# Row sums and root steps kept in PSUM, GpSimd's order written out in one stage, and the opening's order of work changed, in a three-layer float32 block on one core

## The chip, the cores and the metric

The kernel runs on one core of a Trainium2 chip. The metric is the device time of one execution in microseconds. Three executions of the kernel before took 1303.06, 1309.24 and 1313.09 us; their median is 1309.24 us. A further execution was recorded by the hardware profiler.

The core has five engines that run side by side: PE (TensorE, matrix products, which write to the accumulator memory PSUM), DVE (VectorE), ACT (ScalarE), POOL (GpSimd, which works in the main on-chip memory SBUF alone) and SP (SyncE, which here only issues the loads and stores). Each takes its own instructions strictly one after the other, so an instruction that waits holds up all that is queued behind it on its engine.

## The reference, cut to what matters

512 tokens of width 1024 pass through one block of a first model and two layers of a second, all in float32:

```
h = rms_norm(x);  proj = h @ w_in                       # 3 kinds of keys and values, queries, gates
y_attn = (compressed + selected + window attention) @ w_attn_br
y_conv = silu(layer_norm(conv31(a * sigmoid(gate)))) @ w_conv_br
x = x + (g_a * y_attn + g_b * y_conv) @ w_out           # g_a, g_b: sigmoid gates, 2 x 1024 wide
x = x + (silu(conv3(u_a)) * conv3(u_v)) @ w_down        # u = rms_norm(x) @ w_up, 2 x 2816 wide
x = rms_norm(x)
layer 0: x = x + gate * even_mixer(rms_norm(x) * (1 + scale) + shift)   # dense + latent attention
layer 1: x = x + gate * odd_mixer(rms_norm(x) * (1 + scale) + shift)    # window of 128, sinks
out = rms_norm(x)
```

Every rms_norm and layer_norm needs, for each token, the sum of 1024 (or 512) squares and 1/sqrt of it.

## The kernel before, in words

**Layout.** The tokens lie along the free dimension: x is held as eight tiles X[0..7] of 128 features by 512 tokens. A tile of 512 float32 in each of the 128 partitions fills one PSUM bank; there are eight banks, in the pools pg (2), ps (2), pt (3) and po (1).

**Products.** PE multiplies numbers that are split in two: a rounded high part (ACT copies it) and a low part, the difference (POOL or DVE subtracts). `wload` (line 100) loads a weight tile over SP's queue into a raw buffer (pools t and wr), makes its high part at line 110 on ACT and its low part at line 111 on POOL or DVE; the list `wpools` says which raw pool and which engine come next in turn. `mm3` (line 121) then issues three products for each of the eight steps along the contracted dimension: low weight times high x (line 124), high times low (125), high times high (126), all added up in one bank.

**Squares and roots.** `Squares` (line 198) takes eight tiles. ACT squares each one into an SBUF tile (line 222), DVE adds them up in an SBUF buffer z one behind (lines 212 and 215), and `sums` lets PE add the 128 features of each token by products with a column of ones (line 232): one product for 128 tokens of the sum, and one for the last square. DVE reads these few columns at line 183 and `newton` (line 160) makes 1/sqrt in eight more small instructions (lines 164 to 173), each of which needs the one before. All of its operands lie in SBUF. `row_bcast` (line 186) spreads the result over the partitions with PE (line 189). There are twelve such roots: one for the first norm (line 346), one for the layer_norm (698), one for the second norm (722), two by halves of the tokens in the first model's last product (853), two for queries and keys (923), one for the latents (942), two in layer 0's last product (1127), two in layer 1's (1232).

**What sets the order.** The program is traced in the order of the text, and a scheduler decides each engine's order by simulated times and free buffers. `in_order(...)` (line 281) pins the named engines to the order of the text; `after_root()` and `after()` put a block's instructions behind a given one on its engine. Loads are issued by SP in the scheduler's order and wait in that queue for a free buffer.

**The opening** (lines 321 to 355): for each k ACT makes the high part of X[k], DVE the low part; four tiles of the first weights w0 are loaded in between; ACT's order is pinned. Then ACT squares the eight tiles. PE, pinned as well, does the two products pkv[0] and pkv[1], then half of pkb[0] (four steps), the sums of squares, the rest of pkb[0], the broadcast of the root, and pkb[1]. Line 437 takes pkb out of its banks, in the text behind `windows(tkv[0])`, which is a row of copies on ACT, DVE and POOL. The next products (line 453, `natural`) need a free ps bank, which pkb holds, and the weights wv, eight tiles whose low parts are made by POOL, DVE, POOL in turn (line 425).

**The gates** (lines 643 to 684): behind the first model's attention, PE multiplies by the sixteen gate weights, each two tiles of `wload` with the low part on POOL. In the same stage the convolution's 31 taps go on: three channel tiles on DVE, and tile 0 on POOL, one addition at line 488 for each tap, of a copy that ACT makes at line 487. Sixteen taps of tile 0 are left for this stage, spread over fourteen gates in the text. PE and DVE are pinned here, POOL is not.

**By halves** (`by_halves`, line 796): in the last product of each model's layers, tokens 0 to 255 are finished first and their root is made while PE works on tokens 256 to 511. Evacuations of the second half stand behind the first half's root on DVE.

Of the kernel before, what the change touches and what calls it, by code (L numbers as in the profile page):

```python
# [18 lines left out]
D = 1024  # L19
# [24 lines left out]
def build(ctx, tc, I, out):  # L44
# [49 lines left out]
    V.memset(ones, 1.0)  # L94


    wpools = [[("t", "wh", "wl", G), ("t", "wh", "wl", V), ("wr", "wh", "wl", G)]]
# [22 lines left out]

    def mm3(ps, ls, rs, start=True, stop=True):
        n = len(ls)
        for i, ((lh, ll), (rh, rl)) in enumerate(zip(ls, rs)):
            PE.matmul(ps, ll, rh, start=start and i == 0, stop=False)  # L124
            PE.matmul(ps, lh, rl, start=False, stop=False)  # L125
            PE.matmul(ps, lh, rh, start=False, stop=stop and i == n - 1)  # L126
# [32 lines left out]

    def newton(x):  # L160
        n = x.shape[1]
        y = new("s", (128, 20))[:, :n]
        t = new("s", (128, 20))[:, :n]
        V.tensor_scalar(y.bitcast(I32), x.bitcast(I32), -0.5, float(0x5F3759DF), op0=OP.mult, op1=OP.add)


        V.tensor_mul(t, y, y)
        V.scalar_tensor_tensor(t, t, -0.5 * 0.375, x, op0=OP.mult, op1=OP.mult)
        V.scalar_tensor_tensor(y, t, 1.5 * 0.375, y, op0=OP.add, op1=OP.mult)
        V.tensor_mul(t, y, y)  # L170
        V.scalar_tensor_tensor(t, t, 64.0 / 9, x, op0=OP.mult, op1=OP.mult)
        V.scalar_tensor_tensor(t, t, -10.0 / 3, t, op0=OP.add, op1=OP.mult)
        root[:] = [V.scalar_tensor_tensor(y, t, 5.0, y, op0=OP.add, op1=OP.mult)]
        return y

# [4 lines left out]

    def rsqrt(src, scale, eps):
        x = new("s", (128, 20))[:, :src.shape[1]]
        V.tensor_scalar(x, src, scale, eps, op0=OP.mult, op1=OP.add)
        return newton(x)

# [7 lines left out]
    def to_sbuf(ps, tag="R"):  # L193
        t = new("r", tag=tag)
        V.tensor_copy(t, ps)
        return t

    class Squares:


        def __init__(self, a=0, b=512):
            self.c = slice(a, b)
            self.acc = self.last = None
# [15 lines left out]

        def add(self, src, scale=1.0):  # L220
            t = new("p")
            A.activation(t[:, self.c], src[:, self.c], AF.Square, scale=scale)  # L222
            self.put(t)

        def sums(self, bank="ps"):
            st = new(bank)
            n = (self.c.stop - self.c.start) // 128
            for x in (self.acc, self.last):
                for i in range(n):

                    a = self.c.start + 128 * i
                    PE.matmul(st[:, i:i + 1], x[:, a:a + 128], ones[:, 0:1], start=x is self.acc and i == 0,  # L232
                              stop=x is self.last, skip_group_check=True)
            return st[:, 0:n]

# [106 lines left out]
    with in_order("PE"):  # L342
        for b in range(2):
            mm3(pkv[b], w0[8 * b:8 * b + 8], xg)
        mm3(pkb[0], wk[0][:4], xg[:4], True, False)
        r1 = rsqrt(total.sums("pt"), 1.0 / D, EPS)
        mm3(pkb[0], wk[0][4:], xg[4:], False, True)
        R1 = to_sbuf(row_bcast(r1, "pt"))
# [3 lines left out]
    for b in range(2):  # L352
        t = new("p")
        V.tensor_mul(t, pkv[b], R1)
        tkv.append(t)
# [67 lines left out]
    KB = []  # L423
    with after_root():
        wv = wsplit(I["w_v"], KT, 280, ("m", "h"))
    nc.sync.dma_start(vec[:, 8:NVEC], I["vec"][:, 8:NVEC])
# [3 lines left out]
    w2h, w2l = split(w2r, shape=(128, 128), p="z")  # L430
    w2k, w2v = [(w2h[:, i:i + 64], w2l[:, i:i + 64]) for i in (0, 64)]
    with after_root():
        ZK = windows(tkv[0], cv("pek", 0, 16))
    tkb = []
    for b in range(2):
        tkb.append(new("p"))
        V.tensor_mul(tkb[b], pkb[b], R1)
    with after_root():
# [244 lines left out]
    with in_order("PE", "DVE"):  # L683
        gates(0, 7, 0, 90)
        total = Squares()
# [5 lines left out]
        PE.matmul(mp, ones, total.last, start=False, stop=True)  # L691
        total = Squares()
        for c in range(4):
# [23 lines left out]
    for m in range(KT):  # L717
# [3 lines left out]
        total.add(X[m])  # L721
    R2 = to_sbuf(row_bcast(rsqrt(total.sums(), 1.0 / D, EPS), "po"), "R'")

# [122 lines left out]
    for th, c in by_halves(I["w_dn"], 18, 22, ACTV[18:], down, "t", ws):  # L846
# [5 lines left out]
        V.scalar_tensor_tensor(v[:, 2:4], st[:, 1], 1.0 / D, t, op0=OP.mult, op1=OP.add)  # L852
        R = row_bcast(newton(v), "pt")
        r0 = new("r", tag=("R", "R'")[th])[:, 0:256]
# [60 lines left out]
    for i in range(4):  # L915
# [6 lines left out]
        if i % 2:  # L922
            rs = rsqrt(ss[:, 10 * i - 10:10 * i + 10], 1.0, EPS)
            for z in range(2):
# [6 lines left out]
    def latent_inputs(w):  # L931
        ss = new("s", (128, 16))[:, 0:8]
        for i in range(4):
# [7 lines left out]
            CN.append(cn)  # L941
        rc = rsqrt(ss, 1.0, EPS)
        for i, cn in enumerate(CN):
# [182 lines left out]
    for th, c in by_halves(I["w_eo"], 4, 8, OC[4:], attn_out, "m", ws):  # L1126
        R = row_bcast(rsqrt(sums[th].sums(), 1.0 / D, EPS), "pt")
        for k in range(KT):
# [102 lines left out]
    for th, c in by_halves(I["w_oo"], 4, 8, OC[4:], last_out, "m", ws):  # L1231
        R = row_bcast(rsqrt(sums[th].sums(), 1.0 / D, EPS), "pt")
        r0 = new("r", tag=("R", "R'")[th])[:, 0:256]
# [139 lines left out]
```

## Time and profile before

| what | value |
|---|---|
| median of three executions | 1309.24 us (1303.06 to 1313.09) |
| the profiled execution, its own time | 1305.09 us |
| its span, first to last instruction | 1303.1 us |
| PE busy | 1248.2 us, 96% of the span |
| DVE, ACT, POOL busy | 893.2, 701.7, 729.7 us (69%, 54%, 56%) |
| mean granted TensorE clock | 0.992 of full speed |
| loads and stores | 124.74 MB, mean 96 GB/s |

An engine counts as busy from an instruction's start to its end, pipelined products overlap, and waits stand outside. The granted clock is a share of 2.4 GHz. All durations in rows below come from this one execution.

### The profile page before, as it was taken

To read this page: it belongs to the slowest core of one execution; us is meant where nothing else is said; L and a number is where in the kernel's file an instruction comes from. 1 tells how busy PE (TensorE), PEld (TensorE's weight loads), DVE (VectorE), ACT (ScalarE), POOL (GpSimd) and SP (SyncE) were. 2 spreads that over 40 slices of the span, in tenths; PEclk is the share of its full clock that TensorE was granted. 3 is DMA by queue.
4 is the path that set the end of the run, shared out by engine and by line. 5 is a ranking of instruction groups with operands and counts; after the bars stand their busy time and mean duration, and the time that the engine had idled before them with its cause. 6 is when DMAs were issued, how large, how long until landed. Compare 5 with 4: busy or idle time off the path is not lost. (4 is left out here: it accounts for less than half of the span.)

```text
span 1303.1 us, 19296 instructions
## 1 busy us (share of the span) xinstructions
PE 1248.2 (96%) x6369; PEld 1039.2 (80%) x6369; DVE 893.2 (69%) x1967; ACT 701.7 (54%) x1487; POOL 729.7 (56%) x715
## 2 busy tenths in 40 slices
PE   7899999799999999999999999999999989999996
PEld 5878877688888888888888798877777788888886
DVE  7755767697645777776877358677787776655565
ACT  6756777334543444423443243586677646776654
POOL 4457785844644666565665513477565423676542
PEclk9999999899999999999999999999999999999998
DMA  6231011332443555587553501211111111111221
GB/s 209 78 97 58 33 59 33 122 98 87 124 123 97 161 170 161 163 252 240 165 162 87 160 16 40 72 39 50 47 60 42 41 50 57 57 57 57 67 72 65
DMA packets 71971, 124.74 MB, mean 96 GB/s; under 512 B 8256, under 2 KB 17344, under 8 KB 71872
## 3 DMA queue, kind: packets, MB, share of 16 engines
q1 hardware_dynamic: 71872, 123.52, 30.5%
q8 instruction: 50, 0.82, 0.3%
q14 instruction: 49, 0.40, 0.1%
HBM read 121.39 MB, written 2.10 MB: 95 GB/s over the span
## 5 line engine op out<-in xcount | busy, mean ns | idle before, releaser
L111 POOL TENSOR_TENSOR wl<-wr,wh 128x512 fp32r<-128x512 f32 (+2 forms) x215 | 281.9, 1314 | 266.7 <-ACT wh L110 208.9
L124 PE MATMUL pg<-h,wl 128*128 128x512 f32 x628 | 249.3, 397 | 2.8 <-POOL wl L111 2.7
L126 PE MATMUL pg<-h,wh 128*128 128x512 f32 x628 | 246.7, 393 | 0.0
L125 PE MATMUL pg<-h,wh 128*128 128x512 f32 x628 | 246.5, 393 | 0.0
L110 ACT ACTIVATE wh<-wr 128x512 fp32r<-128x512 f32 (+2 forms) x215 | 132.5, 618 | 174.9 <-PE pg L126 83.0
L124 PEld LDWEIGHTS pg<-h,wl 128*128 128x128 f32 x628 | 118.4, 188 | 26.6 <-POOL wl L111 4.1
L126 PEld LDWEIGHTS pg<-h,wh 128*128 128x128 f32 x628 | 118.4, 189 | 23.0
L125 PEld LDWEIGHTS pg<-h,wh 128*128 128x128 f32 x628 | 118.5, 189 | 22.2 <-issue 0.7
L111 POOL TENSOR_TENSOR m<-t,m 128x512 fp32r<-128x512 f32 (+1 forms) x67 | 89.5, 1336 | 80.4 <-ACT m L110 78.3
L304 DVE TENSOR_TENSOR t<-pt,t 128x512 fp32r<-128x512 f32 (+1 forms) x160 | 97.4, 631 | 27.0 <-ACT t L303 25.8
L309 PE MATMUL po<-t,h 128*128 128x512 f32 (+3 forms) x384 | 110.0, 364 | 4.3 <-DVE t L304 1.9
L124 PE MATMUL ps<-h,wl 128*128 128x512 f32 x260 | 103.4, 398 | 7.4 <-POOL wl L111 7.4
L126 PE MATMUL ps<-h,wh 128*128 128x512 f32 x260 | 102.0, 392 | 0.0
L125 PE MATMUL ps<-h,wh 128*128 128x512 f32 x260 | 102.0, 392 | 0.0
L303 ACT ACTIVATE t<-pt 128x512 fp32r<-128x512 f32 (+1 forms) x160 | 84.4, 552 | 22.8 <-PE pt L299 22.1
L309 PEld LDWEIGHTS po<-t,h 128*128 128x128 f32 x384 | 65.7, 188 | 28.8 <-ACT t L303 13.2
L299 PE MATMUL pt<-k,p 128*128 128x128 f32 x576 | 85.5, 273 | 2.7 <-POOL p L976 2.5
L299 PEld LDWEIGHTS pt<-k,p 128*128 128x128 f32 x576 | 69.0, 140 | 14.3 <-POOL p L976 5.0
L744 DVE CUSTOM_DVE_ANT_0 b<-b,z 128x512 f32<-128x512 f32 x48 | 75.4, 1572 | 0.0
L976 POOL TENSOR_SCALAR p<-p,s 128x512 f32<-128x512 f32 x64 | 45.5, 713 | 49.8 <-DVE s L975 49.7
L124 PEld LDWEIGHTS ps<-h,wl 128*128 128x128 f32 x260 | 49.2, 189 | 20.2 <-POOL wl L111 10.1
L110 ACT ACTIVATE m<-t 128x512 fp32r<-128x512 f32 (+2 forms) x78 | 46.9, 604 | 33.7 <-PE ps L124 12.9
(404 smaller groups left out, 3050.9 us busy)
## 6 DMA issues: line engine op xcount, KB each, us to landing
b<-ada_t SPq DMA_DIRECT2D x48, 256.0 KB, 3.2
z<-ada_t SPq DMA_DIRECT2D x48, 256.0 KB, 3.2
t<-w_up SPq DMA_DIRECT2D x44, 256.0 KB, 2.8
wr<-w_up SPq DMA_DIRECT2D x44, 256.0 KB, 2.7
wr<-w_g SPq DMA_DIRECT2D x32, 256.0 KB, 2.6
t<-w_dn SPq DMA_DIRECT2D x23, 256.0 KB, 2.7
wr<-w_br SPq DMA_DIRECT2D x16, 256.0 KB, 2.7
wr<-w_gt SPq DMA_DIRECT2D x16, 256.0 KB, 2.8
```

The costliest lines, as they stand in the source:

```text
L110: A.activation(hi[:, :z], raw[:, :z], AF.Copy)
L111: eng.tensor_sub(lo[:, :z], raw[:, :z], f(hi[:, :z]))
L124: PE.matmul(ps, ll, rh, start=start and i == 0, stop=False)
L125: PE.matmul(ps, lh, rl, start=False, stop=False)
L126: PE.matmul(ps, lh, rh, start=False, stop=stop and i == n - 1)
L299: PE.transpose(ps[:, o:o + 128], src, ident)
L303: evac[:] = [A.activation(hi[:, :n], ps[:, :n], AF.Copy)]
L304: evac.append(V.tensor_sub(lo[:, :n], ps[:, :n], f(hi[:, :n])))
L309: PE.matmul(o[:, a:b], v, t[:, pa:pa + b - a], start=start and z == 0, stop=stop and z == 1)
L744: V.tensor_tensor_reduce(out=raw, in0=raw, in1=CA[z], op0=OP.mult, op1=OP.add, scale=1.0, scalar=0.0, accum_out=MA[l][:, z, m:m + 1])
L976: scaled[0] = G.tensor_scalar(p, p, sm[:, 1:2], 0.0, op0=OP.mult, op1=OP.add)
```

## The change

- `Squares.add` no longer keeps its running sum in SBUF. The first square is written by ACT into a PSUM bank (pool pt), each further one is added to it there by DVE at once, and the one before the last is added into the SBUF buffer z, so that PE can read the sum. `of` says how many squares come.
- `newton` keeps its values y and t in spare columns (64 and up) of a PSUM bank: the one that holds the sums, or one handed in. So that no instruction has two operands in PSUM, r, q and u are kept in SBUF: the start value and the first step are computed twice, once for PSUM and once for SBUF, and one fused step becomes two. It has eleven instructions in place of eight.
- The bank of the sums becomes pt at the second norm and po in the halves of layers 0 and 1; roots of lines 923 and 942 get a bank of po of their own.
- The gates 0 to 6 are traced under `in_order("Pool")`: POOL is pinned there to the order of the text.
- Opening: ACT copies one column of ones at the very beginning; the first product takes high times high, high times low, low times high; pkb[0] has two steps ahead of the sums, not four; wv's low parts are all made on POOL, with raw buffers from t and wr in turn, and no longer stand behind the root; pkb[0] is taken out of its bank ahead of `windows(tkv[0])`, which stands behind that, and pkb[1] behind it.

```
+    A.activation(new("s", (128, 1)), ones[:, 0:1], AF.Copy)
...
-    def mm3(ps, ls, rs, start=True, stop=True):
+    def mm3(ps, ls, rs, start=True, stop=True, early=False):
         n = len(ls)
+        if early:
+
+            for i, ((lh, ll), (rh, rl)) in enumerate(zip(ls, rs)):
+                PE.matmul(ps, lh, rh, start=start and i == 0, stop=False)
+                PE.matmul(ps, lh, rl, start=False, stop=False)
+                PE.matmul(ps, ll, rh, start=False, stop=stop and i == n - 1)
+            return
...
-    def newton(x):
+    def newton(x, bank=None):
+
         n = x.shape[1]
-        y = new("s", (128, 20))[:, :n]
-        t = new("s", (128, 20))[:, :n]
-        V.tensor_scalar(y.bitcast(I32), x.bitcast(I32), -0.5, float(0x5F3759DF), op0=OP.mult, op1=OP.add)
-
-
-        V.tensor_mul(t, y, y)
+        r, q, u = [new("s", (128, 20))[:, :n] for _ in range(3)]
+        st = bank or work[0]
+        y = st[:, 64:64 + n]
+        t = st[:, 128:128 + n]
+        for z in (y, r):
+            V.tensor_scalar(z.bitcast(I32), x.bitcast(I32), -0.5, float(0x5F3759DF), op0=OP.mult, op1=OP.add)
+
+
+        V.tensor_mul(t, y, r)
         V.scalar_tensor_tensor(t, t, -0.5 * 0.375, x, op0=OP.mult, op1=OP.mult)
-        V.scalar_tensor_tensor(y, t, 1.5 * 0.375, y, op0=OP.add, op1=OP.mult)
-        V.tensor_mul(t, y, y)
+        for z in (y, q):
+            V.scalar_tensor_tensor(z, t, 1.5 * 0.375, r, op0=OP.add, op1=OP.mult)
+        V.tensor_mul(t, y, q)
         V.scalar_tensor_tensor(t, t, 64.0 / 9, x, op0=OP.mult, op1=OP.mult)
-        V.scalar_tensor_tensor(t, t, -10.0 / 3, t, op0=OP.add, op1=OP.mult)
-        root[:] = [V.scalar_tensor_tensor(y, t, 5.0, y, op0=OP.add, op1=OP.mult)]
-        return y
+        V.tensor_scalar(u, t, -10.0 / 3, None, op0=OP.add)
+        V.tensor_mul(t, t, u)
+        root[:] = [V.scalar_tensor_tensor(r, t, 5.0, q, op0=OP.add, op1=OP.mult)]
+        return r
...
-        def add(self, src, scale=1.0):
+        def add(self, src, scale=1.0, bank="pt"):
+
+            i, c = self.n, self.c
+            self.n += 1
+            if i == 0:
+                self.sum = new(bank)
+                A.activation(self.sum[:, c], src[:, c], AF.Square, scale=scale)
+                return
             t = new("p")
-            A.activation(t[:, self.c], src[:, self.c], AF.Square, scale=scale)
-            self.put(t)
+            A.activation(t[:, c], src[:, c], AF.Square, scale=scale)
+            if i == self.of - 1:
+                self.last = t
+            else:
+                acc = self.sum
+                if i == self.of - 2:
+                    self.acc = new("z", (128, 542))[:, 0:512]
+                    acc = self.acc
+                V.tensor_add(acc[:, c], self.sum[:, c], t[:, c])
+            return t
...
-            mm3(pkv[b], w0[8 * b:8 * b + 8], xg)
-        mm3(pkb[0], wk[0][:4], xg[:4], True, False)
+            mm3(pkv[b], w0[8 * b:8 * b + 8], xg, early=b == 0)
+        mm3(pkb[0], wk[0][:2], xg[:2], True, False)
         r1 = rsqrt(total.sums("pt"), 1.0 / D, EPS)
-        mm3(pkb[0], wk[0][4:], xg[4:], False, True)
+        mm3(pkb[0], wk[0][2:], xg[2:], False, True)
...
-        V.tensor_mul(t, pkv[b], R1)
+        root[:] = [V.tensor_mul(t, pkv[b], R1)]
...
-    with after_root():
-        wv = wsplit(I["w_v"], KT, 280, ("m", "h"))
+    wpools[0] = [("t", "wh", "wl", G), ("wr", "wh", "wl", G)]
+    wv = wsplit(I["w_v"], KT, 280, ("m", "h"))
+    wpools[0] = [("t", "wh", "wl", G), ("t", "wh", "wl", V), ("wr", "wh", "wl", G)]
...
+    tkb = [new("p") for _ in range(2)]
+    root[:] = [V.tensor_mul(tkb[0], pkb[0], R1)]
     with after_root():
         ZK = windows(tkv[0], cv("pek", 0, 16))
-    tkb = []
-    for b in range(2):
-        tkb.append(new("p"))
-        V.tensor_mul(tkb[b], pkb[b], R1)
+    V.tensor_mul(tkb[1], pkb[1], R1)
...
-        gates(0, 7, 0, 90)
+        with in_order("Pool"):
+            gates(0, 7, 0, 90)
...
-        total = Squares()
+        total = Squares(of=4)
...
-    R2 = to_sbuf(row_bcast(rsqrt(total.sums(), 1.0 / D, EPS), "po"), "R'")
+    R2 = to_sbuf(row_bcast(rsqrt(total.sums("pt"), 1.0 / D, EPS), "po"), "R'")
...
-        R = row_bcast(newton(v), "pt")
+        R = row_bcast(newton(v, sums[th].st), "pt")
...
-            rs = rsqrt(ss[:, 10 * i - 10:10 * i + 10], 1.0, EPS)
+            rs = rsqrt(ss[:, 10 * i - 10:10 * i + 10], 1.0, EPS, new("po"))
...
-        rc = rsqrt(ss, 1.0, EPS)
+        rc = rsqrt(ss, 1.0, EPS, new("po"))
...
-        R = row_bcast(rsqrt(sums[th].sums(), 1.0 / D, EPS), "pt")
+        R = row_bcast(rsqrt(sums[th].sums("po"), 1.0 / D, EPS), "pt")
```

The last pair of lines stands twice, at lines 1127 and 1232. `rsqrt` hands its new argument on to `newton`, and `sums` notes its bank in the list `work`.

## Rows read from the trace of the kernel before

**Rows 1.** The page's list of busy time, share of the span and instructions.

```profile
PE 1248.2 (96%) x6369; PEld 1039.2 (80%) x6369; DVE 893.2 (69%) x1967; ACT 701.7 (54%) x1487; POOL 729.7 (56%) x715
```

**Rows 2.** PE's waits, whole span: line <- releaser: us in total, times, longest.

```profile
PE pg L124 <- DVE m L111: 7.3, 1, 7.3
PE pt L189 <- DVE s L173: 5.4, 5, 2.1
PE ps L124 <- DVE p L437: 3.4, 1, 3.4
PE ps L232 <- DVE z L215: 3.4, 3, 2.1
...
PE po L189 <- DVE s L173: 1.0, 1, 1.0
```

**Rows 3.** PE's waits in the gates' stage, 230 to 260 us.

```profile
PE ps L124 <- POOL wl L111: 4.1, 2, 3.5
PE pg L124 <- POOL wl L111: 2.7, 2, 2.2
```

**Rows 4.** Mean granted TensorE clock (behind PE's to POOL's busy times) of three stretches.

```profile
20.00:60.00 40.00, 34.52 (x201) 30.76 (x200) 30.31 (x65) 24.30 (x57) 23.54 (x31) 0.96 0.30 89
...
200.00:300.00 100.00, 93.08 (x410) 75.02 (x411) 76.59 (x128) 48.79 (x89) 61.16 (x52) 0.97 0.28 88
...
1040.00:1100.00 60.00, 55.65 (x370) 51.23 (x369) 44.35 (x98) 29.10 (x61) 17.39 (x14) 0.97 0.17 54
```

**Rows 5.** Timeline of the opening: start us, us, engine, line, what [idle before].

```profile
3.81 1.28 ACT L330 ACT_TABLE_LOAD   x1 [3.81 <-DMA k<-vec]
...
7.27 0.79 PE L124 MATMUL pg<-h,m 128*128 128x512 f32 x1 [7.27 <-DVE m L111]
...
10.11 0.63 ACT L110 ACTIVATE m<-t 128x512 fp32r<-128x512 f32 x1 [0.18 <-DMA t<-w_q]
...
13.84 0.74 DVE L331 SCALAR_TENSOR_TENSOR h<-x,k,h 128x512 fp32r<-128x512 f32 x1
...
14.74 0.39 PE L124 MATMUL pg<-h,m 128*128 128x512 f32 x1
```

**Rows 6.** Timeline: last step of the first root; first products with wv.

```profile
29.62 0.70 DVE L173 SCALAR_TENSOR_TENSOR s<-s,s 128x4 f32<-128x4 f32 x1
...
40.39 0.57 PE L124 MATMUL ps<-m,h 128*128 128x280 f32 x1 [3.40 <-DVE p L437]
```

**Rows 7.** Timeline, POOL and DVE, at the second norm's root.

```profile
406.29 1.30 POOL L111 TENSOR_TENSOR m<-t,m 128x512 fp32r<-128x512 f32 x1 [2.62 <-ACT m L110]
...
406.40 1.20 DVE L169 SCALAR_TENSOR_TENSOR s<-s,s 128x4 f32<-128x4 f32 x1
```

**Rows 8.** Timeline of the very last root, with POOL idle.

```profile
1293.74 0.16 DVE L183 TENSOR_SCALAR s<-ps 128x2 f32<-128x2 f32 x1 [1.15 <-PE ps L232]
...
1295.31 0.16 DVE L173 SCALAR_TENSOR_TENSOR s<-s,s 128x2 f32<-128x2 f32 x1
```

**Rows 9.** DVE groups by form, whole span: count | busy us, mean ns | idle before.

```profile
L842 DVE TENSOR_TENSOR x<-x,ps 128x256 f32<-128x256 f32 x8 | 3.4, 419 | 5.6 <-PE ps L126 5.6
...
L678 DVE TENSOR_TENSOR ps<-ps,m 128x512 f32<-128x512 f32 x2 | 1.4, 700 | 0.1
...
L212 DVE TENSOR_TENSOR z<-h,h 128x512 f32<-128x512 f32 x1 | 0.7, 684 | 0.0
```

**Rows 10.** Timeline of the gates' stage: POOL, ACT, PE.

```profile
231.27 5.37 POOL L488 TENSOR_TENSOR h<-h,t 128x512 f32<-128x512 f32 x4
...
217.17 1.32 ACT L487 ACTIVATE t<-z,k 128x512 f32<-128x512 f32 x2
...
217.02 0.39 PE L124 MATMUL pg<-h,wl 128*128 128x512 f32 x1
...
237.91 0.69 PE L124 MATMUL ps<-h,wl 128*128 128x512 f32 x1 [3.50 <-POOL wl L111]
```

**Rows 11.** Timeline in layer 0's last product: DVE adds a square while POOL works.

```profile
1044.82 1.39 DVE L215 TENSOR_TENSOR z<-z,p 128x256 f32<-128x256 f32 x1
```

More of the change, by code (lines that the diff above doesn't have):

```diff
@@ L179, in after_root, with rsqrt @@
         return tc.issue_after(getattr(root[0], "ins", root[0]))
-    def rsqrt(src, scale, eps):
+    def rsqrt(src, scale, eps, bank=None):
         x = new("s", (128, 20))[:, :src.shape[1]]
         V.tensor_scalar(x, src, scale, eps, op0=OP.mult, op1=OP.add)
-        return newton(x)
+        return newton(x, bank)
     def row_bcast(col, tag="ps"):
@@ L196, in to_sbuf, with __init__ @@
         return t
+    work = []
     class Squares:
-        def __init__(self, a=0, b=512):
-            self.c = slice(a, b)
+        def __init__(self, a=0, b=512, of=KT):
+            self.c, self.of, self.n = slice(a, b), of, 0
             self.acc = self.last = None
@@ L233, in sums @@
                               stop=x is self.last, skip_group_check=True)
+            work[:] = [st]
             return st[:, 0:n]
@@ L1231, in build @@
     for th, c in by_halves(I["w_oo"], 4, 8, OC[4:], last_out, "m", ws):
-        R = row_bcast(rsqrt(sums[th].sums(), 1.0 / D, EPS), "pt")
+        R = row_bcast(rsqrt(sums[th].sums("po"), 1.0 / D, EPS), "pt")
         r0 = new("r", tag=("R", "R'")[th])[:, 0:256]
```

## The prediction

> **What bounds the kernel now.** I read the busy times first. PE is busy for 1248.2 us of a span of 1303.1 [rows 1]: the kernel is a stream of products, and only PE's 55 idle us, and slow clock, are to be had from an edit that removes no product. So next the waits of PE by releaser [rows 2]. The reader should see that four of the five largest are touched here: the start (7.3), a root's last step (5.4 in five places, 2.1 of it in one, and 1.0 at the second norm), the bank that line 437 frees (3.4), the sums of squares (3.4). The same view, cut to the gates' stage, adds 6.8: weights whose low part POOL was late with [rows 3]. Third, the granted clock by stretch [rows 4]. It is 1.00 elsewhere in the middle of the kernel and below it in the three stretches where these long waits lie; behind a wait the products run for some us at the lower level, 1.2 GHz. A share of 0.96 over 40 us is 1.6 us of work lost, 0.97 over 100 us is 3.0, 0.97 over 60 us is 1.8. So each of those waits costs half as much again. Last, timelines around each wait, to see why it is there.
>
> One of them explains most of the change. POOL begins a subtraction of two SBUF tiles at 406.29 and needs 1.30 us; a DVE step on four columns, both operands in SBUF, begins at 406.40 and ends when POOL does, 1.20 us where it otherwise takes 0.16 [rows 7, 8]. The first root's last step took 0.70 [rows 6]; an addition of squares 1.39 [rows 11], against 0.42 for a like one with an operand in PSUM [rows 9]. An operand in PSUM takes DVE out of POOL's way.
>
> **The change part by part.** All against the profiled execution, 1305.1 us, which stands 4.1 below the median of three (1309.2).
>
> *Opening.* ACT's table load takes 1.28 us after the first load has landed [rows 5]; the copy of one column puts it into idle time. High times high needs no low part. PE could so start up to 2.2 us ahead of 7.27: 1.28, and about 0.9 for the low part of the weights and the wait for it (an estimate: one DVE subtraction, 0.68 to 0.74). But ACT waits for a load at 10.11 already, so its earlier start doesn't last, and PE's step for the last x tile, at 14.74, comes just behind that tile's low part, 13.84 + 0.74 = 14.58 [rows 5]. Of that step only the first product can go ahead. I take -0.4; ends 0 and -2.2.
>
> *First root, R1, wv.* Two steps ahead of the sums in place of four bring the root forward by six products, and leave 18 behind the sums to cover it: at 0.227 us each (93.08 us of busy PE by 410 products, the middle row of [rows 4]) 4.1 us, more than the root needs. PE's 2.1 us there go. Line 437's evacuation no longer queues behind wv's subtractions and the window copies on DVE: the 3.4 us before 40.39 [rows 2, 6] go, and with them the slow clock, 1.6 [rows 4]. Sum -7.1. Against it: wv's three DVE subtractions move to POOL, and four of its eight loads, not two, now take one of the three wr buffers, so that SP's queue holds them until POOL has released earlier ones, and behind them in that queue stand the vectors, the second constants and the query weights. What covers this is that PE wants wv only behind pkb[1], some ten us later. What is late next is ACT, which must empty the first of wv's banks while it still copies windows. I give back 1.1: -6. Ends -3 and -7.1.
>
> *Gates.* Four additions of taps ran in one piece for 5.37 us while weights waited behind them; PE stood for 3.50 before 237.91 [rows 10]. In the text's order there is about one tap between two gates: POOL's work is then 2 x 1.3 + 1.34 = 4.0 us a gate, against 24 products x 0.227 = 5.45 on PE. The 6.8 us and 3.0 of clock [rows 3, 4] go: -9.8. Behind the pinned order something new is late: the second gate's weights, until now prepared far ahead, stand behind the first tap, whose copy ACT makes at 217.17, two in 1.32, the first ready at 217.9. Then 1.34 for the tap and 1.3 for the weights give 220.6; PE began that gate at 217.02 [rows 10]. A new wait of 3.6 us, and clock at the ratio of this stage, 3.0 / 6.8 x 3.6 = 1.6. I take -9.8 + 5.2 = -4.6. Ends: -9.8 if ACT copies earlier, +39 if every gate waits as long as that one (below).
>
> *Roots.* A step undisturbed takes (1295.31 - 1293.74) / 8 = 0.196 us from start to start [rows 8]. The new chain has ten steps that wait for each other, not nine (line 183 counted), and two more instructions that wait for nothing new, each between nothing and 0.2: I take 0.1. What a step costs when it writes PSUM, no row shows at this width. From below: reading PSUM costs nothing (0.16 at line 183 and 0.16 at 173). From above: 0.700 against 0.68 to 0.69 for a full tile that only reads it [rows 8, 9], +0.02. Six such steps: +0.1. So an undisturbed root gets dearer by 0.2 + 0.2 + 0.1 = 0.5, and one that POOL struck as in [rows 7] cheaper by 1.04 - 0.5 = 0.5. The Trainium skill, Perfetto Trace Analysis, Optimizing Scalar/DVE Operations, puts DVE's overhead per instruction at about 60 ns on SBUF and 125 on PSUM, which would speak against the change; the 0.16 us for both at lines 183 and 173 doesn't bear that out for a read. Of the waits at a root [rows 2] 2.1 is counted above; of the other 3.3 I put half at the halves of the first model's product, where POOL works (-0.5 each), half at the very end, where it is idle (+0.5 each). The second norm gets -0.5 of its 1.0. Sum -0.5; ends -2.5 and +3. The other roots PE does not wait for. The bank of line 698's sums is now held through the root, about 2 us longer, out of four wide ones: covered, since PE works on one and has two more.
>
> *Squares.* The adds take 0.42, whatever POOL does. PE's waits for the sums, 3.4, lie where adds of up to 1.39 [rows 2, 11] chain with the evacuations behind them on DVE. I take -2.4 and half of that stretch's 1.8 of clock: -3.3. Ends 0 and -5.2. The pool pt gives one of three banks to a sum; where this happens no transposes run.
>
> Sum: -0.4 - 6 - 4.6 - 0.5 - 3.3 = -14.8. 1305.1 - 14.8 = 1290.3 in the profiled execution's terms, 1309.2 - 14.8 = **1294.4** in the median's.
>
> **Rivals.**
>
> *Half is given back.* An earlier PE finds the next engine late: ACT's window copies in the opening (-3 of it stays), two new waits in the gates in place of one (-9.8 + 2 x 5.2, so +0.6), squares -3, opening and roots -0.5 together. Sum -5.9: 1303. For it: the scheduler, whose simulated times know nothing of POOL and DVE blocking each other, orders everything anew. Against: POOL has idle time in both places.
>
> *All of it.* ACT copies taps early, nothing else is late: -1.3 - 7.1 - 9.8 - 1.5 - 5.2 = -24.9, so 1284. Against: ACT copied the first tap as soon as splits of the attention's output were out of its way.
>
> *PSUM steps are dear.* If each of about nine instructions that touch PSUM in a root costs another 0.2 (a whole step), five roots on the path cost 5 x 1.8 = 9: 1303. This is the skill's rule, taken larger than its page has it; by its own figures (65 ns) it is 3 us, 1297. Little for it in [rows 8].
>
> *Slower: a pinned POOL that starves PE at every gate.* POOL's order has a tap behind each gate's weights; the tap needs ACT's copy, ACT may stand at a high part whose load waits for a raw buffer that only POOL's next subtraction frees. Priced by the one wait seen, 3.5 us at 14 gates is 49, of which 9.8 is there already: +39, less the 10.2 of the other parts: about 1338. It decides from 1.5 us a gate. Against it: three raw buffers and 1.4 us of slack a gate.
>
> **How the numbers follow.** A difference under 1%, 13.1 us, can't be told from none. Forecast 0.50, its own range 1288 to 1300, of which about 0.36 lies below 1296; half 0.22 (1300 to 1307); all 0.12; dear PSUM steps 0.06; starved gates 0.10. Faster: 0.36 + 0.12 = 0.48. Slower 0.10 less a little for a mild case, with as much from the unknown new order: 0.10. Same: 0.42. The range, 1284 to 1308, leaves out the starved gates and the ends of all and half.
>
> **What would show it.** Right: no wait of PE at lines 189 and 124 between 25 and 45 us and the clock there at 1.00; one wait for line 111 at the second gate and none behind; root steps of 0.2 us beside a busy POOL; adds of 0.42. Wrong: PE waiting at line 124 for POOL in several gates; root steps above 0.3; PE's first product at 6 us and the last x step still at 14.7 shows only that the opening gave nothing. The sum fails if the waits move to ACT, at line 455 or 487.

## The result, and the profile after

The changed kernel takes 1298.01 us (median of nine runs, 1296.26 to 1303.06). The kernel before, run beside it, takes 1305.26 as a median of nine; the 1309.24 of the prediction was three of these. The ratio is 0.9933, 95% interval 0.9913 to 0.9954: 0.7% faster, 7.3 us between the medians and 8.7 by the ratio, where the forecast said 14.8 (1.1%). 1298.0 lies in the range, but 4.0 of the 11.2 us down from 1309.24 are the median of before having come down. By the ratio the forecast was too large, and the rival "half is given back" (5.9 us) is nearer than the likeliest case.

The page's busy times of the changed kernel, which answer to [rows 1]:

```profile
PE 1251.2 (96%) x6369; PEld 1041.1 (80%) x6369; DVE 883.7 (68%) x2000; ACT 701.9 (54%) x1488; POOL 730.1 (56%) x718
```

DVE has 9.5 us less to do, and PE is busy no less. PE's waits in the changed kernel (line <- releaser: us, times, longest), to be held against [rows 2, 3]:

```profile
PE pg L128 <- ACT m L112: 6.3, 1, 6.3
PE pg L133 <- POOL wl L113: 3.9, 2, 3.7
PE ps L133 <- POOL wl L113: 3.2, 4, 1.5
PE po L264 <- DVE z L254: 3.0, 2, 2.8
...
PE pt L204 <- DVE s L188: 2.3, 1, 2.3
PE ps L133 <- DVE x L1156: 2.0, 1, 2.0
PE pg L133 <- ACT p L488: 1.9, 1, 1.9
```

Lines 133 and 128 are the products, 204 the broadcast of a root (189 before), 264 the sums (232 before). The roots' waits fell from 5.4 and 1.0 to one of 2.3, at the very end. The 3.4 before wv is gone. But three long waits are new or longer: 3.7 for POOL at 218 us, 1.9 for ACT at 49 us, 2.0 for a bank at 1059 us (1.4 before); and the wait for z is not 2.1 but 2.8. The stretches of [rows 4] again, with the granted clock behind the five busy times:

```profile
20.00:60.00 40.00, 38.12 (x230) 34.20 (x229) 28.45 (x68) 28.02 (x63) 28.07 (x36) 0.96 0.30 91
200.00:300.00 100.00, 96.14 (x424) 78.39 (x423) 80.41 (x126) 48.96 (x84) 65.39 (x53) 0.97 0.34 100
1040.00:1100.00 60.00, 54.36 (x339) 49.38 (x338) 39.50 (x105) 26.51 (x57) 15.04 (x12) 0.94 0.17 54
```

The clock is no better than before in any of them: in this execution it falls behind each of the new waits. It need not. The changed kernel run again (e1) waits 2.01 us at the same products at 48.65 and shows a clock of 1.00 from 49 to 54 us, where this execution shows 0.66.

**A ledger.** PE multiplies the same 2,544,656 columns in every version. So I add up columns along each trace and ask when a version has done as many as before had at a given time; the difference of these lags over a stretch is what the stretch won (-) or lost (+), waits and clock together. Stretches are in time of the kernel before, those with little in them are left out; the runs are described below.

| stretch, us | changed | again (e1) | no pin (e2) | old opening (e3) | root in SBUF (e4) | squares in SBUF (e5) | pin alone (f1) |
|---|---|---|---|---|---|---|---|
| 0-20, start | +0.8 | -0.3 | +0.7 | +0.2 | +0.8 | -0.3 | +0.4 |
| 20-50, first root, wv | -7.4 | -7.4 | -7.4 | -3.7 | -5.6 | -6.6 | +0.5 |
| 50-205 | +3.7 | +2.3 | +3.8 | +0.2 | +1.0 | +4.1 | +0.2 |
| 205-222, second gate | +6.8 | +6.9 | 0.0 | +5.6 | +6.7 | +5.6 | +5.7 |
| 222-270, other gates | -11.2 | -11.2 | -1.6 | -11.2 | -11.2 | -11.2 | -11.2 |
| 270-340, layer_norm's sums | +2.2 | +2.2 | +2.3 | +0.7 | +2.2 | 0.0 | 0.0 |
| 340-440, second norm | -0.3 | -0.4 | -0.3 | -0.5 | +1.4 | -1.2 | 0.0 |
| 765-800, first model's halves | -2.0 | -2.0 | -2.0 | -2.0 | 0.0 | -2.0 | 0.0 |
| 800-890 | +1.5 | +1.6 | +1.5 | +1.6 | -0.1 | +1.5 | 0.0 |
| 1035-1090, layer 0's halves | +3.2 | +3.1 | +1.7 | +3.4 | -0.4 | +3.2 | +1.4 |
| 1240-1291, layer 1's halves | -0.9 | -0.9 | -0.9 | -0.9 | -0.6 | -0.3 | 0.0 |
| all, to 1291 | -3.5 | -6.3 | -2.7 | -7.2 | -6.0 | -7.4 | -3.3 |

One execution carries 2 to 3 us of chance in its start and its clock. The first two columns, one kernel twice, differ by 1.4 us at 50-205, where the clock fell in one execution only. At 1035-1090 the last column shows +1.4 although its code there is that of before. So times are taken from the medians and places from this table.

### The profile page after: what moved, and what is told of

It reads as the page before. It is cut to its first block, busy times and chain, and to the rows that moved or that the text cites. A ratio compares the mean times of both kernels' runs of the same rounds, so it can differ in the third digit from the quotient of the medians.

```text
span 1299.5 us, 19323 instructions
## 1 busy us (share of the span) xinstructions
PE 1251.2 (96%) x6369; PEld 1041.1 (80%) x6369; DVE 883.7 (68%) x2000; ACT 701.9 (54%) x1488; POOL 730.1 (56%) x718
```

## The experiments

All kernels ran in five rounds beside the kernel before; ratios are to it, with their 95% intervals.

| run | median us | ratio | interval |
|---|---|---|---|
| e1, changed again | 1298.39 | 0.9940 | 0.9918 to 0.9962 |
| e2, no pin | 1302.96 | 0.9972 | 0.9958 to 0.9986 |
| e3, old opening | 1298.40 | 0.9935 | 0.9909 to 0.9960 |
| e4, root in SBUF | 1296.48 | 0.9921 | 0.9901 to 0.9941 |
| e5, squares in SBUF | 1298.54 | 0.9940 | 0.9920 to 0.9960 |
| e6, taps later | 1293.28 | 0.9897 | 0.9874 to 0.9920 |
| e7, wv's banks first | 1306.06 | 0.9996 | 0.9979 to 1.0013 |
| e8, e6 and e7 | 1300.08 | 0.9948 | 0.9930 to 0.9967 |
| f1, before, pin alone | 1300.87 | 0.9948 | 0.9932 to 0.9963 |
| f2, e6, stacked keys later | 1291.80 | 0.9878 | 0.9861 to 0.9895 |
| f3, f2, PSUM only beside POOL | 1289.20 | 0.9872 | 0.9847 to 0.9897 |
| f4, f3, w_ok's copies later | 1287.88 | 0.9849 | 0.9820 to 0.9879 |

**The changed kernel again.** No edit.

> The changed kernel once more, unaltered, to see which of its waits stand in a second recorded execution. Theory A, the order of the instructions makes them: PE's 3.7 us before the second gate's products at about 218 us, its 1.9 us at about 49 us for ACT, its 2.8 and 2.0 us at about 1046 and 1059 us return to within 0.3 us each, and the last x step of the first product starts again at 14.9 us. Theory B, part of it is the luck of one execution: the opening's loads land differently, that step starts at 14.1 to 14.6 us, and the slow stretch behind the 0.5 us wait at 311 us is gone; then this execution is 2 to 4 us shorter than the 1301.3 us of the first one. Both: 1296 to 1299 us as median, 0.993 of the kernel before.

Waits of 3.7, 2.0, 2.7 and 2.0 us came back at the same products, so the waits belong to the order of the instructions (A). The slow clock came back behind the wait at the layer_norm's sums (+2.2 in both columns) and not behind the one at 49 us (+2.3 in place of +3.7): it belongs in part to the execution. The start differs by 1.1 us with the same order of loads, and lies between -0.3 and +0.8 in all versions that have the new one: there B holds.

**One part undone.** e2:

```
-        with in_order("Pool"):
-            gates(0, 7, 0, 90)
+        gates(0, 7, 0, 90)
```

> The changed kernel without POOL pinned to the text in the gates' stage. Theory A, the prediction's gates term (9.8 us of waits and slow clock removed, 5.2 us added at the second gate, net -4.6; the two traces say -11.2 and +6.8, net -4.4): the weights' waits between 228 and 252 us return, the one at 218 goes, and the kernel takes 4 to 5 us longer than the changed one, about 1302.5 us, 0.997 of before. Rival B, the pinned order gives back all it wins: 1297 to 1299 us, as the changed kernel. Rival C, the order matters through the clock alone and costs more, +8 us or more: 1306.

4.6 to 5.0 us longer: A. At the second gate the stretch shows 0.0 in place of +6.8, behind it -1.6 in place of -11.2. POOL's waits of [rows 3] are back (4.4 and 2.7 us); the 1.6 is the clock, which fell once there and not twice (0.96 from 222 to 270 us, 0.93 before). e3 takes back the opening's edits:

```
-    A.activation(new("s", (128, 1)), ones[:, 0:1], AF.Copy)
-            mm3(pkv[b], w0[8 * b:8 * b + 8], xg, early=b == 0)
+            mm3(pkv[b], w0[8 * b:8 * b + 8], xg)
-        mm3(pkb[0], wk[0][:2], xg[:2], True, False)
+        mm3(pkb[0], wk[0][:4], xg[:4], True, False)
...
-    wpools[0] = [("t", "wh", "wl", G), ("wr", "wh", "wl", G)]
-    wv = wsplit(I["w_v"], KT, 280, ("m", "h"))
+    with after_root():
+        wv = wsplit(I["w_v"], KT, 280, ("m", "h"))
...
```

> The changed kernel with the opening of the kernel before: no early copy on ACT, low times high first in the first product, four steps ahead of the sums, wv's low parts with DVE's turn and behind the root, pkb taken out behind the first windows; sums, roots, squares and the pinned POOL stay new. Theory A, the ledger of the two traces (start +0.8, root and wv -7.4, ACT late for wv's banks +3.7, together -2.9): 2 to 4 us longer than the changed kernel, about 1301 us, with PE's wait before wv at 40 us back at about 3 us and the wait at 49 us for ACT gone. Rival B, the prediction's -6.4 was right and the 3.7 us came from elsewhere: about 1304.4 us. Rival C, the opening's gain came from the root and sums in PSUM alone: 1297 to 1299 us, and no wait at 40 us.

The median is the changed kernel's to within 0.4 us: C in the time, though not in the place. PE's wait before wv is back with the 3.40 us of [rows 6], and the 1.9 us for ACT don't follow it. The clock stays at 1.00 behind it here (37 to 45 us), as it did not before; that much of the -3.7 is this one execution's luck. PE's longest waits at these two points, first in e3, then in the changed kernel:

```profile
38.27 0.37 PE L132 MATMUL ps<-m,h 128*128 128x280 f32 x1 [3.40 <-DVE p L469]
```

```profile
49.56 0.48 PE L133 MATMUL pg<-h,wl 128*128 128x512 f32 x1 [1.88 <-ACT p L488]
```

The opening's edits moved a wait by eleven us. e4 puts `newton` back to its eight instructions, all operands in SBUF (the function of before, word for word):

> The changed kernel with the old root of eight instructions, all of whose operands lie in SBUF; the squares stay in PSUM. Theory A, the prediction's term for the roots (0.5 us dearer where POOL rests, up to 1 us cheaper where it works, net -0.5): within 1.5 us of the changed kernel; the very last root takes 0.5 us less from its first step to its last (1.7 us in place of 2.2), and one or more roots beside a busy POOL show a step of 0.7 us or more. Rival B, steps on PSUM are dear: 3 to 9 us faster than the changed kernel, 1289 to 1295 us. Rival C, POOL's blocking is the larger part: 2 to 4 us slower, 1300 to 1302 us.

1.5 to 1.9 us faster, intervals overlapping: at the edge of A (within 1.5), short of B (3 to 9), and not for B's reason. What one step costs is seen best where POOL's subtraction meets the root of the second norm, as in [rows 7]. The changed kernel, DVE and POOL, and then e4:

```profile
402.16 1.29 POOL L113 TENSOR_TENSOR m<-t,m 128x512 fp32r<-128x512 f32 x1 [2.59 <-DMA wr<-w_up]
...
402.39 0.17 DVE L181 SCALAR_TENSOR_TENSOR pt<-pt,s 128x4 f32<-128x4 f32 x1
```

```profile
401.70 1.30 POOL L113 TENSOR_TENSOR m<-t,m 128x512 fp32r<-128x512 f32 x1 [1.88 <-issue]
...
401.86 1.15 DVE L177 SCALAR_TENSOR_TENSOR s<-s,s 128x4 f32<-128x4 f32 x1
```

With one operand in PSUM the step runs beside POOL in 0.17 us; with both in SBUF it ends when POOL ends. In the first root, beside wv's subtractions on POOL, e4's last four steps take 0.70 to 0.74 us each and PE waits 1.5 for them; the changed kernel's last step is done at 27.98 and PE doesn't wait:

```profile
28.43 0.72 DVE L180 SCALAR_TENSOR_TENSOR s<-s,s 128x4 f32<-128x4 f32 x1
29.18 0.70 DVE L181 SCALAR_TENSOR_TENSOR s<-s 128x4 f32<-128x4 f32 x1
29.91 0.70 DVE L182 SCALAR_TENSOR_TENSOR s<-s,s 128x4 f32<-128x4 f32 x1
```

```profile
27.82 0.16 DVE L188 SCALAR_TENSOR_TENSOR s<-pt,s 128x4 f32<-128x4 f32 x1
```

So the mechanism holds, and it is worth something at 20 to 50 (1.8 us between the columns), at the second norm (1.7 us between the columns) and in the first model's halves (2.0, of which 1.5 come back by 890). Where POOL is idle it loses: 3.6 us lie between the columns at 1035 to 1090, though the size varies there from one execution to the next (f3). e5 puts the squares' sum back in SBUF (the class of before):

> The changed kernel with the old sums of squares, added up in SBUF one behind; roots stay in PSUM, POOL pinned, opening new. Theory A, the prediction's squares term (-3.3 us at PE's waits for the last addition): 2 to 4.5 us longer than the changed kernel, about 1301.3 us, with additions of 0.8 to 1.4 us beside a busy POOL and PE's waits for z back to 3 us or more. Rival B, the ledger of the two traces (the stretch from 1040 to 1090 us is 3.2 us longer with the squares in PSUM): 2 to 3.5 us shorter than the changed kernel, about 1295 us. Rival C, the sums never set the time, only the order of ACT's instructions around them does: within 1.5 us.

The medians agree to within 0.5 us: C in the time, though intervals of some 2.6 us to either side leave room for part of A. The additions do get shorter; the 20 of 256 columns in e5, and in the changed kernel (count | busy us, mean ns | idle before):

```profile
L232 DVE TENSOR_TENSOR z<-z,p 128x256 f32<-128x256 f32 x20 | 12.1, 606 | 4.2 <-ACT p L239 3.9
```

```profile
L254 DVE TENSOR_TENSOR pt<-pt,p 128x256 f32<-128x256 f32 x20 | 8.5, 427 | 2.6 <-ACT p L246 2.2
```

DVE saves 0.18 us a time. In layer 0's halves PE's wait for z goes back to the 3 us and more that A names, and for A's reason: DVE's additions, lengthened beside POOL, stand between the evacuations that ACT's squares wait for. PE's wait in e5 (1030 to 1090 us), and one of these additions:

```profile
PE po L249 <- DVE z L232: 3.8, 1, 3.8
```

```profile
1034.22 1.39 DVE L232 TENSOR_TENSOR z<-z,p 128x256 f32<-128x256 f32 x1
```

The changed kernel waits 2.8 us there, and for another reason. What ACT does ahead of that wait:

```profile
1041.13 0.81 ACT L246 ACTIVATE p<-x 128x256 f32<-128x256 f32 x2 [1.34 <-DVE x L1156]
1044.35 0.63 ACT L112 ACTIVATE wh<-wr 128x512 fp32r<-128x512 f32 x1 [2.40 <-DMA wr<-w_ok]
1044.88 0.40 ACT L246 ACTIVATE p<-x 128x256 f32<-128x256 f32 x1
```

The seventh square, 0.40 us long, stands behind a copy of a weight that hasn't landed, and that PE first uses at 1076.7. At the layer_norm and at the second norm, too, the changed kernel makes PE wait for a square of ACT's, 0.50 and 0.7 us; e5 waits at neither. What PSUM takes from DVE's additions, ACT's new order gives back.

**The two new waits.** e6 moves the taps:

```
+            k, n = max(i - 2, 0), len(todo) - 2
-            for t in rest[len(rest) * i // len(todo):len(rest) * (i + 1) // len(todo)]:
+            for t in rest[len(rest) * k // n:len(rest) * (k + 1) // n] if i > 1 else []:
                 conv_tap(0, t)
```

> The changed kernel with the first tap on POOL behind the third gate's weights in the text, sixteen taps over twelve gates in place of fourteen, POOL pinned as before. Theory A, the second gate's weights were late only because the first tap stood ahead of them on POOL: PE's 3.7 us at 218 us and the slow clock behind them (3.1 us) go, nothing comes in their place; 6 to 7 us shorter than the changed kernel, about 1291.3 us, 0.988 of before. Rival B, the shortage moves on: with 4/3 taps a gate POOL needs 4.4 us of 5.45, but the taps wait for ACT's copies one gate later and PE waits 2 to 4 us at the third or fourth gate: 1295 to 1298 us. Rival C, the loads are late and not POOL: the 3.7 us stay, 1297 to 1299 us.

5 us shorter where A said 6 to 7, and A's 0.988 lies in the interval; the second gate shows 0.0, the gates behind it still -11.2, and between 200 and 262 us PE waits nowhere. POOL in the changed kernel, then in e6:

```profile
215.10 1.66 POOL L521 TENSOR_TENSOR h<-h,t 128x512 f32<-128x512 f32 x1 [10.62 <-ACT t L520]
216.72 2.52 POOL L113 TENSOR_TENSOR wl<-wr,wh 128x512 fp32r<-128x512 f32 x2
```

```profile
214.67 3.09 POOL L113 TENSOR_TENSOR wl<-wr,wh 128x512 fp32r<-128x512 f32 x2 [10.46 <-ACT wh L112]
217.70 1.31 POOL L521 TENSOR_TENSOR h<-h,t 128x512 f32<-128x512 f32 x1
```

One tap of 1.66 us ahead of the weights, with POOL idle for 10.6 before it, was 6.8 us of PE. In e7 the loop that empties wv's banks stands ahead of the second windows, which are put behind its last copy:

```
-    with after_root():
-        ZV = windows(tkv[1], cv("pev", 0, 16))
-    for t in tkb:
-        KB.append([stack_k(t, 0), stack_k(t, 64)])
...
-        A.activation(t[:, 0:280], ps[:, 0:280], AF.Copy, scale=r1[:, i:i + 1])
+        last = A.activation(t[:, 0:280], ps[:, 0:280], AF.Copy, scale=r1[:, i:i + 1])
...
+    with tc.issue_after(getattr(last, "ins", last)):
+        ZV = windows(tkv[1], cv("pev", 0, 16))
+    for t in tkb:
+        KB.append([stack_k(t, 0), stack_k(t, 64)])
```

> The changed kernel with ACT emptying wv's four banks ahead of its copies for the second windows and the stacked keys. Theory A, PE's 1.9 us at 49 us and the slow clock behind it come from ACT's order alone: both go, 3 to 4 us shorter than the changed kernel, about 1294.5 us, 0.990 of before. Rival B, the second windows are then late for the products that need them and PE waits there instead, near 90 us: 1297 to 1299 us.

8 us slower, worse than either theory. The wait at 49 us goes; ACT in e7:

```profile
41.52 0.49 ACT L484 ACTIVATE p<-pg,s 128x280 f32<-128x280 f32 x1 [2.01 <-PE pg L135]
...
47.66 0.49 ACT L484 ACTIVATE p<-pg,s 128x280 f32<-128x280 f32 x1 [2.01 <-PE pg L135]
...
56.99 0.42 ACT L430 ACTIVATE wh<-wr 128x256 fp32r<-128x256 f32 x1
```

and PE's waits behind it, from 50 to 80 us:

```profile
PE pg L434 <- POOL wh L431: 3.4, 1, 3.4
PE pg L434 <- POOL wl L431: 2.4, 1, 2.4
```

ACT stands three times 2.0 us for a bank that PE hasn't filled, and the weights of line 434, behind all this, are late. That is near B, a wait moved on to what comes next, but it is the weights that are late and not the windows, near 60 us and not 90, and the price is higher than that of the wait removed.

> Both of the last two edits in one kernel. If both theories A hold and don't touch each other, their gains add: 9 to 11 us shorter than the changed kernel, about 1287.8 us, 0.985 to 0.987 of before. If one of them fails, the sum is what the other alone gave.

1300.08 us: e6's 5 us won and e7's 8 lost, add up to within about 1 us; its ledger shows both, 0.0 at the second gate and +10.1 between 58 and 205.

**Do the parts add?** Undone one by one (against 1298.2, the mean of the changed kernel's two medians) they come to +4.8, +0.2, -1.7 and +0.3 us, 3.6 together and not 7.3; each has an interval of some 2 to 3 us to either side. f1 puts the pin alone into the kernel before.

> The kernel before with nothing but POOL pinned to the text for gates 0 to 6. Theory A: the pin's worth doesn't depend on the rest. The stage from 205 to 270 us shows +5.6 to +6.8 us at the second gate and -11.2 behind it, net -4.4 to -5.6 us: about 1301 us, 0.996 of before; the other three parts together then make the remaining 3 us, though each of them alone can be undone at no cost. Rival B, the single undoings add: opening 0, squares 0, root in PSUM -1.7 (better without), so the pin is the whole change: 1297 to 1299 us, 0.9935.

0.9948 where all four parts give 0.9933 to 0.9940. With +5.7 and -11.2 the place is A's; the time doesn't decide, since the interval holds A's 0.996 and B's 0.9935. The pin is most of the change. The other three alone give 0.9972 (e2), and on top of the pin 1 to 2 us, which the intervals don't tell from nothing.

**A better version.** f2 leaves ACT the second windows first, then wv's banks, and puts the stacked keys behind the weights of line 434:

```
-    for t in tkb:
-        KB.append([stack_k(t, 0), stack_k(t, 64)])
...
     hk = compressed(ZK, I["cmp_k_w1"])
+    with after_root():
+        for t in tkb:
+            KB.append([stack_k(t, 0), stack_k(t, 64)])
```

(`compressed` notes each copy of a weight in `root`.)

> The changed kernel with the later taps, and ACT's copies for the stacked keys put behind the weights of the first compressed product, so that ACT empties wv's banks right behind the second windows and never waits for a bank that isn't full. Theory A, the 1.9 us wait at 49 us and the slow clock behind it go and the compressed product's weights are not late: 3 to 4 us shorter than the kernel with the later taps alone (1293.3), about 1289.8 us, 0.9873 of before. Rival B, as when all four banks were emptied first, PE only meets the next late thing, the weights at line 434: 1293 us or more.

1.5 us shorter than e6, between the two theories, and the intervals overlap. At 58 us PE is 7.1 us ahead of before (2.9 in the changed kernel), at 205 us 4.1: 3.1 are lost between, at one wait of 1.6 us for line 436's copy on ACT and the slow clock next to it. f3 uses the old `newton` in lines 1127 and 1232 of before and the old squares for the layer_norm.

> The kernel of the run above, and PSUM used only where POOL works beside it: the roots of the layers' halves (lines 1127 and 1232 of before) in SBUF again in eight instructions, the layer_norm's squares in SBUF again. Theory A, the two traces' ledger: 2.2 us at the layer_norm (a 0.5 us wait and slow clock behind it), about 3.4 us between 1055 and 1090 us (PE's 2.0 us wait for a bank that DVE empties behind the longer root, and slow clock), 0.5 us at the end; 5 to 6 us shorter than the run above, 1283 to 1285.5 us, 0.9835 of before. Rival B, those differences were the luck of one execution's clock: 1288 to 1291 us.

0.0 in place of +2.3 at the layer_norm, as A has it. At 1035 to 1090 it is 0.3 less, not 3.4: PE's wait for the bank there is 1.0 in place of 2.0, but with one code f2, e1 and e6 show +1.6, +3.1 and +4.6 in that stretch, so e4's size was partly the luck of the clock (B). The median is 2.6 below f2's, half of what A has and within B's 1288 to 1291, and the intervals overlap. f4:

```
     for m in range(2):
-        ps = gemm(I["w_ok"][m], H)
+        with tc.issue_after(getattr(sums[0].act, "ins", sums[0].act)):
+            w = wsplit(I["w_ok"][m], KT, 128)
+        ps = gemm_bank()
+        mm3(ps, w, H)
```

(`sums[0].act` is the last square of the first half.)

> The kernel of the run f3_best, with ACT's copies of layer 1's key weights w_ok put behind the last square of the first half in layer 0's last product. In the changed kernel and in f3_best ACT stands 2.4 to 2.6 us at the first load of w_ok, and the seventh and eighth squares are queued behind that copy. Theory A, this is why the squares in PSUM won nothing there: PE's wait of 3.0 us for z goes to 0.5 us or less, and the slow clock around it (6.8 us at half) halves or goes; 3 to 5.5 us shorter than f3_best (1289.2), about 1285 us, 0.984 of before. Rival B, the end of that stretch is set by DVE, which must take eight x tiles out of their banks and make eight normalised ones: the z wait goes and the same time comes back at the banks of the second half (line 1122 of before); 1287.5 to 1290.5 us.

1.3 us below f3, intervals overlapping: B. PE's waits there in f4, 1010 to 1075 us:

```profile
PE pt L220 <- DVE s L204: 2.5, 1, 2.5
PE po L280 <- DVE z L270: 0.9, 1, 0.9
```

The 3.0 us for z are 0.9, so ACT's copy was their cause, and 2.5 us stand now at the root. f4 beats both kernels: 1.5% under before (0.9820 to 0.9879) where the change gave 0.7%.

## Why the prediction was right and where it was wrong

*The gates* came out as worked: -4.4 forecast -4.6, with the one new wait at 3.74 us where the sum had 3.6, none behind it, and e2 and e6 moving the time as that says. Both sizes were a little low, 11.2 for 9.8 and 6.8 for 5.2, the second because the clock at the wait cost more than the ratio gave. From 217 to 224 us in the changed kernel:

```profile
217.00:224.00 7.00, 5.96 (x14) 4.71 (x15) 2.59 (x4) 3.08 (x6) 7.00 (x6) 0.51 0.40 115
```

At 0.51 some 3.4 us are lost, where the sum had 1.6. That is one execution again: e3 waits the same 3.74 us and shows 0.76 from 217 to 224 us, 1.7 lost, and its +5.6, like that of e5 and f1, is close to the 5.2.

*First root and wv*: the removed waits are right (-7.4, forecast -7.1), and "what is late next is ACT, which must empty the first of wv's banks" is what happened, at line 488 as feared. The price is the failing size: I gave back 1.1 where 1.9 of wait and 1.8 of clock came (2.3 together in e1, where the clock didn't fall). The reason given for the root was only half of it as well. The 4.1 us of products behind the sums cover a root in PSUM, 3.1 us here (24.86 to 27.98). In SBUF it takes 5.7 us beside POOL (e4, 24.94 to 30.61), and PE still waits 1.5 behind the same products: without PSUM the edit of the opening would not have done it. PE doesn't wait in e3 either, but there POOL is idle from 25.79 to 27.61, through most of the root, so e3 doesn't show what the old opening would have cost beside a busy POOL. The edits of the opening can all be taken back at no cost that the intervals show (e3).

*Start*: -0.4 forecast, -0.3 to +0.8 measured; ACT's first copy is at 3.75 and not 5.1, PE's first product at 6.34 and not 7.27, but ACT then waits 1.18 and 0.97 us for loads: the end 0 of the bounds.

*Roots*: the price of a step is right. The last one takes 2.06 us from its first step's start to its last's, 1.57 before [rows 8]: +0.49, forecast 0.5. (The row that the bound took for a full tile that only reads PSUM, line 212, has both operands in SBUF; the steps below measure it.) The first and the last step of that root:

```profile
1289.57 0.16 DVE L198 TENSOR_SCALAR s<-po 128x2 f32<-128x2 f32 x1 [1.15 <-PE po L264]
...
1291.63 0.16 DVE L188 SCALAR_TENSOR_TENSOR s<-po,s 128x2 f32<-128x2 f32 x1
```

A step that writes PSUM takes 168 ns in the roots of the halves, one that only reads it 159, and one with all operands in SBUF 160 to 162 (e4) (count | busy us, mean ns | idle before):

```profile
L183 DVE SCALAR_TENSOR_TENSOR po<-po,s 128x2 f32<-128x2 f32 x4 | 0.7, 168 | 0.1
...
L183 DVE SCALAR_TENSOR_TENSOR s<-po,s 128x2 f32<-128x2 f32 x4 | 0.6, 159 | 0.1
```

The rule of the Trainium skill that was a rival here (Perfetto Trace Analysis, Optimizing Scalar/DVE Operations: about 60 ns on SBUF and 125 on PSUM, so 65 more as an estimate) doesn't show in these steps: 9 ns at most. What decides is the rule of the Trainium skill in its page SBUF — State Buffer, Who interferes with whom: a DVE instruction with two SBUF inputs contends with a GpSimd instruction that reads SBUF, one with at most one such input, outside the 2-port modes, doesn't. The steps of 1.15 and 0.17 us above agree. The last section shows an instruction with one such input that was held all the same; no run shows whether it fell under the exception. But "half at the halves" missed that a root 0.5 us longer, where POOL is idle, holds up the banks queued behind it on DVE: PE's wait for line 1156's bank is 2.0 us in the changed kernel, 1.1 in e4 and 1.0 in f3 (1.3 in e5, with the long root too, so the root is not all of it). With e4 faster by 1.7 the term looks like a small loss rather than -0.5; its interval holds both.

*Squares* is the step that failed: forecast -3.3, worth nothing that the medians show (e5). The adds do take 0.42 us whatever POOL does, and the chain that I read in [rows 11] is real, since it comes back in e5. What I put at nothing is what the new order makes late in its place. In layer 0's halves ACT's last squares now stand behind copies that wait for w_ok, and PE waits 2.8 us for z, where it waited 2.1 before. f4 takes these copies away: the wait for z is 0.9, but 2.5 us stand at the root. At the layer_norm's sums the new order even puts a copy that waits for POOL ahead of a square: PE's wait there is 0.50 us, and where the clock falls behind it 2.2 are lost.

So of the forecast 14.8 the pin's 4.6 and most of the root's wait came, the latter through PSUM more than through the opening; 1.2 to 2.6 more than reckoned were given back at ACT's wv banks (e1 and the first execution), and the 3.3 of the squares never came. The slower rival, a POOL that starves every gate, did not happen: one gate of fourteen waited.

## What to carry to other kernels

Pin an engine's order and read what stands first in it: here one instruction that waits for something else, ahead of work that PE needs, cost 6.8 us of the 11.2 that the pin won, and moving it was one edit. Before an engine's work is made cheaper, ask of the instruction that PE waits for what it was itself queued behind. Take out the parts one by one and put one in alone: three of four here could be removed without a change in time that the intervals show. Do not read the clock behind a wait from one execution.

## What was not expected of the hardware

A short wait can cost several times its length through the clock, and need not. The changed kernel waits 0.50 us between the layer_norm's two sums, and runs the next products at the lower level; the same stretch with the squares in SBUF has no wait and stays at full clock. But e3 has the same 0.50 us wait, at 309.63, and stays at full clock behind it, and loses 0.7 where the changed kernel loses 2.2 (changed, then e5, then e3):

```profile
312.00:317.00 5.00, 5.00 (x20) 4.06 (x20) 2.18 (x13) 0.24 (x1) 0.00 (x0) 0.66 0.17 56
```

```profile
312.00:317.00 5.00, 5.00 (x27) 4.26 (x26) 3.81 (x9) 3.55 (x5) 1.30 (x1) 1.00 0.21 63
```

```profile
310.00:315.00 5.00, 5.00 (x31) 4.36 (x31) 3.11 (x14) 1.34 (x2) 1.06 (x2) 1.00 0.20 57
```

0.66 over 5 us is 1.7 us of work, on top of the 0.5. What decides whether the clock falls no run here shows. A DVE instruction with a single SBUF operand can be held by POOL as well. In the first root of the changed kernel a scaling of 16 columns runs as long as POOL's subtraction beside it, and the root's next step, queued behind it, comes 0.5 us late; in e3, where POOL is idle at that point, the same scaling takes 0.16. POOL, then DVE:

```profile
26.71 0.78 POOL L113 TENSOR_TENSOR h<-wr,m 128x280 fp32r<-128x280 f32 x1
...
26.77 0.75 DVE L1233 TENSOR_SCALAR k<-k 128x16 f32<-128x16 f32 x1
...
27.43 0.15 DVE L186 TENSOR_SCALAR s<-pt 128x4 f32<-128x4 f32 x1
```

So a root in PSUM isn't out of POOL's way altogether: what else DVE does between its steps can be caught. And the same order of loads brought PE to 20 us with 1.1 us of difference between two executions, as large as what the start's edits were to win.
